# Two heads share one forward substitution in a gated delta rule, and ScalarE takes over sums of squares and copies

## The chip, the core and the metric

The kernel runs on one core of a Trainium2 chip. The core has a matrix engine (TensorE; PE in the profile, with PEld for its weight loads), VectorE (DVE), ScalarE (ACT), GpSimd (POOL), and SyncE (SP), which here only issues DMAs. Each engine executes its own list of instructions in order and waits for semaphores of the others. The metric is the time of one execution on the device, in microseconds (us); lower is better.

## The reference, cut to what matters

A decoder trunk of two layers over 512 positions of width 1024. Layer 0 mixes positions by a gated delta rule with 8 heads of 128, layer 1 by differential attention; each is followed by an MLP of width 4096. The change touches the gated delta rule alone. There, after a projection, a causal convolution and a SiLU, every head has q, k and v of 512 x 128 and two gates per position:

```python
a_mat = jnp.where(strict, jnp.einsum('bhnik,bhnjk->bhnij', kb, kc) * decay, 0.0)
rhs = jnp.concatenate([vc * bc[..., None], kb * jnp.exp(gcum)[..., None]], axis=-1)
sol = lax.linalg.triangular_solve(eye + a_mat, rhs, left_side=True, lower=True, unit_diagonal=True)
...
def step(state, inp):
    qg_i, qk_i, u_i, w_i, kd_i, gl_i = inp
    v_new = u_i - jnp.einsum('bhck,bhkv->bhcv', w_i, state)
    o_i = jnp.einsum('bhck,bhkv->bhcv', qg_i, state) + jnp.einsum('bhij,bhjv->bhiv', qk_i, v_new)
    state = state * gl_i[..., None, None] + jnp.einsum('bhck,bhcv->bhkv', kd_i, v_new)
    return state, o_i
```

A unit lower triangular system is solved for every chunk of positions, and a recurrence runs over the chunks. q and k are divided by their norms, and the output of each head goes through an RMS norm and a gate before the output projection.

## The kernel before, in words

The residual is held transposed, model dimension on partitions. Matrix products with weights are made as three fp32r products (high x high, high x low, low x high; `three`, lines 299 to 302). ACT rounds a weight tile to its high part (`wh`, line 293), and POOL or DVE makes the low part (`wl`, line 284). One modulation weight tile per two weight tiles is also reduced on DVE in this stage (line 193).

The delta rule works on four chunks of 128 positions per head. One head passes through these steps:

- `proj_head` (line 490): three projections into three banks of tag `j`; the causal convolution of q, k and v (ACT line 481, DVE line 483), SiLU (line 485). The results kT, qT and vT take three of the 9 buffers `cv`.
- `gdn` up to its first yield, first the decay matrix `ex` (lines 524 to 535). k is transposed and copied to `kn` (line 539, 3 buffers). Its sum of squares is made by `sumsq`: one square of 128x512 on ACT (line 518), one reduction on DVE (line 520). From it come the factors `rk` (POOL, line 543) and `sj`. The products k k and k q scaled by them are `bq` (line 558, 6 buffers, two per head).
- The unit triangular 128x128 matrices are inverted by blocks. The diagonal 16x16 blocks of the four chunks, 32 blocks, are compacted into `dc` (line 574). They go through DRAM (`d1`, line 576) into `mt` with one block per partition (line 578). There a forward substitution, 15 steps of a multiply and a subtract on DVE (lines 584 and 586), makes the inverses `xv`. They go through DRAM again (`d2`, line 589; `tc`, line 591) and are spread into `t` (line 593).
- Three doubling levels (16 to 32, 32 to 64, 64 to 128; lines 596 to 639) make the inverse of 128 out of those of 16. They use products on PE with tag `i` (two banks), copies `um` (lines 607 and 624, one buffer) and subtractions on DVE (lines 614, 615, 635 and 638). `t` and its transpose `z` are updated.
- v is transposed and scaled (`vn`, line 648), and q's sum of squares gives `rq`.
- From the first yield to the second, the recurrence over the four chunks (lines 667 to 691) in one bank `r`. Per chunk: `r` from the state (line 676), a product with `z`, the copy `y` to SBUF on DVE (line 681), then the products of `y` with `kn` (line 683, first three chunks) and with the attention part of `bq` (line 684), the output part `o` and the state `st`.
- After the second yield, the norm of `o` and its transposition into `oT`.

The program emits the heads one after the other: `proj_head(h)`, the whole of `gdn(h)` up to the second yield, then the rest of head h-1 (lines 729 to 735). The gate's projections follow (lines 737 and 738). This order isn't that of the engines: the tile framework plans the lists from it when the kernel is built. Among the instructions whose operands and buffers it expects to be ready it takes the earliest of the program first, so work of later heads stands between the steps of earlier ones. A buffer is given to the next tile of its tag when the last reader of the old one is done. All weight and block transfers are issued by SP in one order.

Of the kernel before, what the change touches and what calls it, by code (L numbers as in the profile page):

```python
# [22 lines left out]
H = 8  # L23
# [62 lines left out]
def trunk_kernel(ctx: ExitStack, tc: tile.TileContext, a, outT):  # L86
# [141 lines left out]

    mhalf = cp.tile([P, 8], F32, name="mhalf")
    G.memset(mhalf, -0.5)  # L230
    eye = cp.tile([32, SUB, SUB], F32, name="eye")
    nc.scalar.dma_start(eye, a["eye"])

    FULL, HALVES = slice(0, S), (slice(0, 256), slice(256, 512))
# [271 lines left out]

    m_sub = mask[:, M_L1:M_L1 + P]

    def gdn(h):
        def natural(src, tag="a"):  # L510
            ps = bank(tag)
            for c in range(NT):
# [2 lines left out]

        def sumsq(src, tag):
            sq = big(g_pool, {"sqq": "sqk"}.get(tag, tag), 1)
            A.activation(sq, src, AF.Square)
            ss = col(4, tag)
            V.tensor_reduce(out=ss, in_=v3(sq), axis=AX.X, op=ALU.add)  # L520
            return ss


# [50 lines left out]
        V.tensor_reduce(out=dc, in_=db.rearrange("p (u b c) -> p u c b", u=4, c=SUB), axis=AX.X, op=ALU.add)  # L574
        d1 = dp.tile([4, P, SUB], F32, tag="d1", name=nm("d1"))
        nc.sync.dma_start(d1.rearrange("u p c -> p u c"), dc)
        mt = g_pool.tile([32, SUB, SUB], F32, tag="mt", name=nm("mt"), bufs=2)
        nc.sync.dma_start(mt.rearrange("p r c -> p (r c)"), d1.rearrange("u (b r) c -> (u b) (r c)", r=SUB))
        xv = g_pool.tile([32, SUB, SUB], F32, tag="xv", name=nm("xv"), bufs=2)
        pr = g_pool.tile([32, SUB, SUB], F32, tag="pr", name=nm("pr"), bufs=2)  # L580
        G.tensor_copy(xv, eye)
        for s in range(SUB - 1):
            shp = [32, SUB - 1 - s, s + 1]
            V.tensor_tensor(out=pr[:, s + 1:, :s + 1], in0=mt[:, s, s + 1:].unsqueeze(2).to_broadcast(shp),
                            in1=xv[:, s, :s + 1].unsqueeze(1).to_broadcast(shp), op=ALU.mult)
            V.tensor_tensor(out=xv[:, s + 1:, :s + 1], in0=xv[:, s + 1:, :s + 1], in1=pr[:, s + 1:, :s + 1],
                            op=ALU.subtract)
        d2 = dp.tile([32, SUB * SUB], F32, tag="d2", name=nm("d2"))
        nc.sync.dma_start(d2, xv.rearrange("p r c -> p (r c)"))
        tc_ = g_pool.tile([P, 4, SUB], F32, tag="tc", name=nm("tc"), bufs=2)  # L590
        nc.sync.dma_start(tc_, d2.rearrange("(u b) (r c) -> (b r) u c", u=4, r=SUB))
        t_ = big(g_pool, "t", 2)
# [23 lines left out]
        for b in (32, 64):  # L616
            parts = [(slice(lo, lo + b), slice(lo + b, lo + 2 * b)) for lo in ((0, 64) if b == 32 else (0,))]
            pu = bank("i")
            um = big(g_pool, "um", 1)
            for p0, p1 in parts:  # L620
                for n in range(4):
                    T.matmul(pu[p1, n * b:(n + 1) * b], lhsT=B(n)[p0, p1], rhs=uu(t_, n)[p0, p0], start=True, stop=True)
            for p0, p1 in parts:
                V.tensor_copy(um[p1, 0:4 * b], pu[p1, 0:4 * b])
            pz = bank("i")
            for p0, p1 in parts:
                for n in range(4):
                    T.matmul(pz[p0, n * b:(n + 1) * b], lhsT=um[p1, n * b:(n + 1) * b], rhs=uu(z, n)[p1, p1],
                             start=True, stop=True)
            if b == 32:  # L630
                p0, p1 = parts[0]
                for n in range(4):
                    T.matmul(pz[p1, n * b:(n + 1) * b], lhsT=uu(z, n)[p1, p1], rhs=um[p1, n * b:(n + 1) * b],
                             start=True, stop=True)
                V.tensor_tensor(out=v3(t_)[p1, :, p0], in0=v3(t_)[p1, :, p0],
                                in1=v3(pz[p1, 0:4 * b], b), op=ALU.subtract)
            for p0, p1 in parts:
                V.tensor_tensor(out=v3(z)[p0, :, p1], in0=v3(z)[p0, :, p1], in1=v3(pz[p0, 0:4 * b], b),
                                op=ALU.subtract)
# [27 lines left out]
        for c in range(NT):  # L667
            r = uu(vn, 0)
            if c > 0:
                T.matmul(R(3), lhsT=uu(kT[h], c), rhs=st, start=True, stop=True)  # L670
                if c > 1:
                    out(c - 1)
                else:
                    A.activation(uu(o, 0), R(2), AF.Copy)
                r = g_pool.tile([P, P], F32, tag="r", name=nm("r"), bufs=2)
                V.scalar_tensor_tensor(out=r, in0=R(3), scalar=neg[:, c, h:h + 1], in1=uu(vn, c),
                                       op0=ALU.mult, op1=ALU.add)
                T.matmul(R(1), lhsT=uu(qT[h], c), rhs=st, start=True, stop=True)
            T.matmul(R(2), lhsT=uu(z, c), rhs=r, start=True, stop=True)
            y = g_pool.tile([P, P], F32, tag="y", name=nm("y"), bufs=2)  # L680
            V.tensor_copy(y, R(2))
            if c < NT - 1:
                T.matmul(R(0), lhsT=uu(kn, c), rhs=y, start=True, stop=True)
            T.matmul(R(2), lhsT=ATT(c), rhs=y, start=True, stop=True)
            if c > 0:
                A.activation(uu(o, c), R(1), AF.Copy, scale=eg[:, c, h:h + 1])
            if c == 0:
                V.tensor_copy(st, R(0))
            elif c < NT - 1:
                V.scalar_tensor_tensor(out=st, in0=st, scalar=gl[:, c, h:h + 1], in1=R(0), op0=ALU.mult, op1=ALU.add)  # L690
# [35 lines left out]
        queue[c - 17][1].insert(0, lambda c=c: mod_bias(c - 8, c))  # L726
    rate[0] = 0.5
    heads = []
    for h in range(H):
        proj_head(h)  # L730
        heads.append(gdn(h))
        next(heads[h])
        next(heads[h])
        if h:
            next(heads[h - 1], None)
    rate[0] = 0.5
    for i in range(0, H, 2):
        gate(i, 2)
# [225 lines left out]
def host_inputs(inp):  # L964
    f = {k: np.asarray(v) for k, v in inp.items()}

    def cl(v):
        return v.reshape(-1, P).T

    conv = f["a_conv_w"][0].reshape(4, 24, P).transpose(2, 1, 0).reshape(P, 96)  # L970
    packed = np.concatenate(
        [cl(f["mod_b"]), cl(f["kv_mod_b"]), cl(f["norm_mix_g"]), cl(f["norm_mlp_g"]), cl(f["kv_norm_g"]),
         cl(f["final_g"]), conv, cl(f["a_out_norm_g"]), cl(f["b_subln_g"]), cl(f["b_lambda"])], axis=1)
    assert packed.shape == (P, N_COLS)
    r = {
        "xT": f["x"][0].T,
        "cols": packed,
        "masks": host_masks(),
        "rope": host_rope(),
        "eye": np.tile(np.eye(SUB, dtype=np.float32)[None], (32, 1, 1)),  # L980
        "c": f["c"],
        "a_log": f["a_log"],
        "a_dt_bias": f["a_dt_bias"],
        "mod_wT": f["mod_w"].transpose(0, 2, 1).reshape(12288, D),
        "kv_mod_wT": f["kv_mod_w"].T,
        "a_w_in": f["a_w_in"][0],
        "a_w_out": f["a_w_out"][0],
        "kv_w": f["kv_w"],
        "b_w_q": f["b_w_q"][0],
        "b_w_out": f["b_w_out"][0],  # L990
        "mlp_w1": f["mlp_w1"],
        "mlp_w2": f["mlp_w2"],
    }
    return {k: np.ascontiguousarray(v) for k, v in r.items()}
# [16 lines left out]
```

## Time and profile before

| | |
|---|---|
| median of 3 runs | 1387.76 us (1387.6 to 1387.95) |
| profiled execution, its own time | 1388.69 us |
| its span | 1386.9 us, granted TensorE clock 0.983 |
| PE busy / weight loads | 1314.4 us (95%) / 1112.8 us (80%) |
| DVE, ACT, POOL busy | 851.1, 529.3, 472.0 us |
| stage of the delta-rule heads | from about 70 to 390 us |

A busy PE isn't a PE at its peak: matmuls are pipelined, and the records overlap. A row of a group gives engine, line, operation, tiles and shapes, the count, the busy time in all, the mean of one in ns, and the idle time of the engine before them with what ended it. A row of the timeline begins with start and duration in us. A row of the waits reads: who waited for whom, us in all, times, the longest.

### The profile page before, as it was taken

What the parts mean: (1) busy time and instruction counts of PE and PEld (TensorE: products, weight loads), DVE (VectorE), ACT (ScalarE), POOL (GpSimd) and SP (SyncE); (2) the same over time, 40 slices, a digit from 0 to 9 for tenths busy, and PEclk for the clock granted to TensorE, in tenths of its full rate; (3) what the DMA queues carried; (4) which work ended last, traced back from release to release, by engine and by line L of the source; (5) the groups of instructions that cost most, each with busy time, mean ns of one, the idle gap of its engine ahead of it and who ended that gap; (6) DMA issues with size and microseconds to landing.
All of it is one profiled execution on the core that took longest, in us unless ns stands there. A gap on an engine that the chain in (4) does not pass through costs nothing. (4 is left out here: it accounts for less than half of the span.)

```text
span 1386.9 us, 19590 instructions
## 1 busy us (share of the span) xinstructions
PE 1314.4 (95%) x7432; PEld 1112.8 (80%) x7432; DVE 851.1 (61%) x1688; ACT 529.3 (38%) x951; POOL 472.0 (34%) x281
## 2 busy tenths in 40 slices
PE   4886998999999999999999999999999999999997
PEld 3665887777779888888889988888798888888897
DVE  6989888899856987778861587777552110031113
ACT  3394344443424533225332354444344322143221
POOL 3324132222003544444444112232135444444441
PEclk9997999999999999999999999999999999999998
DMA  9632322224541776766742233211113233232221
GB/s 313 212 88 51 83 77 72 77 73 138 174 165 62 258 242 226 241 233 218 239 169 100 81 99 103 65 65 66 61 62 121 92 97 101 91 105 93 92 76 61
DMA packets 113213, 174.98 MB, mean 126 GB/s; under 512 B 16384, under 2 KB 56992, under 8 KB 113120
## 3 DMA queue, kind: packets, MB, share of 16 engines
q1 hardware_dynamic: 112416, 172.92, 38.7%
q8 instruction: 58, 0.95, 0.3%
q10 hardware_dynamic: 704, 0.83, 0.2%
q14 instruction: 35, 0.29, 0.1%
HBM read 170.04 MB, written 2.62 MB: 124 GB/s over the span
## 5 line engine op out<-in xcount | busy, mean ns | idle before, releaser
L284 POOL TENSOR_TENSOR wl<-raw,wh 128x1024 fp32r<-128x1024 f32 (+1 forms) x137 | 329.6, 2406 | 395.4 <-ACT wh L293 395.4
L293 ACT ACTIVATE wh<-raw 128x1024 fp32r<-128x1024 f32 (+2 forms) x217 | 216.0, 996 | 505.4 <-PE pj L301 253.4
L300 PE MATMUL pj<-h,wh 128*128 128x512 f32 (+1 forms) x816 | 290.7, 360 | 16.4 <-DVE cv L483 7.4
L301 PE MATMUL pj<-h,wh 128*128 128x512 f32 (+1 forms) x816 | 292.0, 358 | 0.0
L302 PE MATMUL pj<-h,wl 128*128 128x512 f32 (+1 forms) x816 | 290.0, 357 | 0.7 <-DVE wl L284 0.7
L193 DVE SCALAR_TENSOR_TENSOR mw<-mw,one,cs 128x1024 f32<-128x1024 f32 x96 | 210.1, 2202 | 47.5 <-ACT one L213 47.2
L300 PEld LDWEIGHTS pj<-h,wh 128*128 128x128 f32 x816 | 155.8, 192 | 37.9 <-ACT h L278 7.9
L302 PE MATMUL pj<-u,wl 128*128 128x512 f32 (+1 forms) x512 | 172.2, 336 | 0.0
L301 PE MATMUL pj<-u,wh 128*128 128x512 f32 (+1 forms) x512 | 172.2, 336 | 0.0
L300 PE MATMUL pj<-u,wh 128*128 128x512 f32 (+1 forms) x512 | 172.1, 336 | 0.0
L302 PEld LDWEIGHTS pj<-h,wl 128*128 128x128 f32 x816 | 156.5, 192 | 19.0 <-DVE wl L284 1.9
L301 PEld LDWEIGHTS pj<-h,wh 128*128 128x128 f32 x816 | 156.8, 192 | 17.9 <-DVE h L279 0.3
L346 DVE SCALAR_TENSOR_TENSOR x<-pj,mod,x 128x256 f32<-128x256 f32 (+1 forms) x53 | 30.3, 585 | 156.0 <-PE pj L302 156.0
L300 PEld LDWEIGHTS pj<-u,wh 128*128 128x128 f32 x512 | 97.2, 190 | 10.3 <-issue 0.2
L301 PEld LDWEIGHTS pj<-u,wh 128*128 128x128 f32 x512 | 97.2, 190 | 10.1
L302 PEld LDWEIGHTS pj<-u,wl 128*128 128x128 f32 x512 | 97.2, 190 | 9.9
L284 DVE TENSOR_TENSOR wl<-raw,wh 128x1024 fp32r<-128x1024 f32 (+2 forms) x80 | 83.7, 1047 | 18.0 <-ACT wh L293 17.9
L767 DVE SCALAR_TENSOR_TENSOR pj<-pj,r 128x512 f32<-128x512 f32 x32 | 21.6, 690 | 52.2 <-ACT r L766 52.0
L300 PE MATMUL pn<-h,wh 128*128 128x512 f32 x128 | 49.8, 389 | 0.0
L301 PE MATMUL pn<-h,wh 128*128 128x512 f32 x128 | 49.8, 389 | 0.0
L302 PE MATMUL pn<-h,wl 128*128 128x512 f32 x128 | 49.8, 389 | 0.0
L300 PE MATMUL pm<-h,wh 128*128 128x512 f32 x128 | 49.8, 389 | 0.0
(298 smaller groups left out, 2377.1 us busy)
## 6 DMA issues: line engine op xcount, KB each, us to landing
raw<-in_mlp_w_dram SPq DMA_DIRECT2D x128, 512.0 KB, 3.6
mw<-in_mod_wT_dram SPq DMA_DIRECT2D x96, 512.0 KB, 4.7
raw<-in_a_w_in_dram SPq DMA_DIRECT2D x96, 128.0 KB, 2.6
mw<-in_kv_mod_wT_dram SPq DMA_DIRECT2D x16, 512.0 KB, 5.1
raw<-in_kv_w_dram SPq DMA_DIRECT2D x16, 512.0 KB, 3.3
x<-in_xT_dram SPq DMA_DIRECT2D x16, 256.0 KB, 5.7
raw<-in_a_w_in_dram SPq DMA_DIRECT2D x16, 256.0 KB, 2.9
raw<-in_a_w_out_dram SPq DMA_DIRECT2D x8, 512.0 KB, 4.3
```

The costliest lines, as they stand in the source:

```text
L193: V.scalar_tensor_tensor(out=w, in0=w, scalar=one, in1=cs, op0=ALU.mult, op1=ALU.mult, accum_out=raw_mod[:, c:c + 1])
L284: (V if n else G).tensor_tensor(out=out, in0=x, in1=hi.bitcast(F32), op=ALU.subtract)
L293: A.activation(wh, raw, AF.Copy)
L300: T.matmul(ps, lhsT=wh, rhs=xh, start=first, stop=False, skip_group_check=skip)
L301: T.matmul(ps, lhsT=wh, rhs=xl, start=False, stop=False, skip_group_check=skip)
L302: T.matmul(ps, lhsT=wl, rhs=xh, start=False, stop=last, skip_group_check=skip)
L346: V.scalar_tensor_tensor(out=x[d][:, sl], in0=ps[j][:, sl], scalar=mod[:, gt + d:gt + d + 1], in1=x[d][:, sl], op0=ALU.mult, op1=ALU.add)
L767: V.scalar_tensor_tensor(out=ps[j], in0=ps[j], scalar=0.0, in1=r, op0=ALU.max, op1=ALU.mult)
```

## The change

Three things change.

The forward substitution leaves `gdn` and becomes `blocks_inv`, once for two heads, on 64 partitions: head h0 writes its blocks to the lower 32 partitions of a common `mt`, head h0+1 to the upper 32. A new first yield stands behind the DMA that fills `mt`. The program's order is now, per pair: projection and first part of the one head, the same of the other, the common substitution, then rest of the first part and recurrence of the one, closing part of the head before it, and the same for the other. Numbers of buffers other than that of `pr` (2 to 1) stay; `eye` has 64 partitions.

`sumsq` makes four squares of 128x128 on ACT, each with an accumulated sum, in place of one square of 128x512 and a reduction on DVE.

The copies `um` of the second and third doubling levels and `y` of the recurrence go from DVE to ACT.

```diff
-    eye = cp.tile([32, SUB, SUB], F32, name="eye")
+    eye = cp.tile([64, SUB, SUB], F32, name="eye")
...
-    def gdn(h):
+    def blocks_inv(inv):
+
+        mt = inv["mt"]
+        xv = inv["xv"] = g_pool.tile([64, SUB, SUB], F32, tag="xv", name=nm("xv"), bufs=2)
+        pr = g_pool.tile([64, SUB, SUB], F32, tag="pr", name=nm("pr"), bufs=1)
+        G.tensor_copy(xv, eye)
+        for s in range(SUB - 1):
+            shp = [64, SUB - 1 - s, s + 1]
+            V.tensor_tensor(out=pr[:, s + 1:, :s + 1], in0=mt[:, s, s + 1:].unsqueeze(2).to_broadcast(shp),
+                            in1=xv[:, s, :s + 1].unsqueeze(1).to_broadcast(shp), op=ALU.mult)
+            V.tensor_tensor(out=xv[:, s + 1:, :s + 1], in0=xv[:, s + 1:, :s + 1], in1=pr[:, s + 1:, :s + 1],
+                            op=ALU.subtract)
+
+    def gdn(h, inv, part):
...
-            A.activation(sq, src, AF.Square)
             ss = col(4, tag)
-            V.tensor_reduce(out=ss, in_=v3(sq), axis=AX.X, op=ALU.add)
+            for c in range(NT):
+                A.activation(uu(sq, c), uu(src, c), AF.Square, accum_out=ss[:, c:c + 1])
...
-        mt = g_pool.tile([32, SUB, SUB], F32, tag="mt", name=nm("mt"), bufs=2)
-        nc.sync.dma_start(mt.rearrange("p r c -> p (r c)"), d1.rearrange("u (b r) c -> (u b) (r c)", r=SUB))
-        xv = g_pool.tile([32, SUB, SUB], F32, tag="xv", name=nm("xv"), bufs=2)
-        pr = g_pool.tile([32, SUB, SUB], F32, tag="pr", name=nm("pr"), bufs=2)
...
+        nc.sync.dma_start(inv["mt"][part].rearrange("p r c -> p (r c)"), d1.rearrange("u (b r) c -> (u b) (r c)", r=SUB))
+        yield
         d2 = dp.tile([32, SUB * SUB], F32, tag="d2", name=nm("d2"))
-        nc.sync.dma_start(d2, xv.rearrange("p r c -> p (r c)"))
+        nc.sync.dma_start(d2, inv["xv"][part].rearrange("p r c -> p (r c)"))
...
-                V.tensor_copy(um[p1, 0:4 * b], pu[p1, 0:4 * b])
+                A.activation(um[p1, 0:4 * b], pu[p1, 0:4 * b], AF.Copy)
...
-            V.tensor_copy(y, R(2))
+            A.activation(y, R(2), AF.Copy)
...
-    for h in range(H):
-        proj_head(h)
-        heads.append(gdn(h))
-        next(heads[h])
-        next(heads[h])
-        if h:
-            next(heads[h - 1], None)
+    for h0 in range(0, H, 2):
+        inv = {"mt": g_pool.tile([64, SUB, SUB], F32, tag="mt", name=nm("mt"), bufs=2)}
+        for h in (h0, h0 + 1):
+            proj_head(h)
+            heads.append(gdn(h, inv, slice(32 * (h - h0), 32 * (h - h0) + 32)))
+            next(heads[h])
+        blocks_inv(inv)
+        for h in (h0, h0 + 1):
+            next(heads[h])
+            next(heads[h])
+            if h:
+                next(heads[h - 1], None)
```

More of the change, by code (lines that the diff above doesn't have):

```diff
@@ L576, in gdn @@
         nc.sync.dma_start(d1.rearrange("u p c -> p u c"), dc)
-        mt = g_pool.tile([32, SUB, SUB], F32, tag="mt", name=nm("mt"), bufs=2)
-        nc.sync.dma_start(mt.rearrange("p r c -> p (r c)"), d1.rearrange("u (b r) c -> (u b) (r c)", r=SUB))
-        xv = g_pool.tile([32, SUB, SUB], F32, tag="xv", name=nm("xv"), bufs=2)
-        pr = g_pool.tile([32, SUB, SUB], F32, tag="pr", name=nm("pr"), bufs=2)
[L581 to L587, printed above, removed]
+        nc.sync.dma_start(inv["mt"][part].rearrange("p r c -> p (r c)"), d1.rearrange("u (b r) c -> (u b) (r c)", r=SUB))
+        yield
         d2 = dp.tile([32, SUB * SUB], F32, tag="d2", name=nm("d2"))
-        nc.sync.dma_start(d2, xv.rearrange("p r c -> p (r c)"))
+        nc.sync.dma_start(d2, inv["xv"][part].rearrange("p r c -> p (r c)"))
         tc_ = g_pool.tile([P, 4, SUB], F32, tag="tc", name=nm("tc"), bufs=2)
@@ L979, in host_inputs @@
         "rope": host_rope(),
-        "eye": np.tile(np.eye(SUB, dtype=np.float32)[None], (32, 1, 1)),
+        "eye": np.tile(np.eye(SUB, dtype=np.float32)[None], (64, 1, 1)),
         "c": f["c"],
```

## The prediction

> **What bounds the kernel now.** I read the totals first, then the sums over stretches.
>
> ```profile
> span 1386.9 us, 19590 instructions
> PE 1314.4 (95%) x7432; PEld 1112.8 (80%) x7432; DVE 851.1 (61%) x1688; ACT 529.3 (38%) x951; POOL 472.0 (34%) x281
> ...
> 70.00:150.00 80.00, 63.42 (x337) 49.25 (x336) 68.66 (x187) 47.75 (x82) 24.17 (x20) 0.87 0.29 79
> 150.00:390.00 240.00, 227.35 (x1559) 184.49 (x1558) 209.29 (x601) 102.78 (x190) 52.03 (x40) 0.99 0.35 102
> 400.00:420.00 20.00, 20.00 (x140) 18.76 (x139) 10.07 (x17) 5.98 (x10) 0.00 (x0) 1.00 0.34 122
> ```
>
> The columns behind each length are PE, PEld, DVE, ACT, POOL, then the granted clock. From 400 us on PE is the bound (20.00 of 20 us in the last row), and the change touches little of what follows. The delta-rule heads run from 70 to about 390 us. There DVE is busy 278 of 320 us (87%), ACT only 151. Time gained or lost is decided in this stage, and it reaches the end in full, since PE has a full queue of work behind it.
>
> PE's 95% from 150 to 390 looks as if 12.7 us were all there is to win. PEld is busy 77% there and 94% from 400 to 420, where PE never waits, so up to 18% of the stage is slack. (The Trainium skill, "Trainium Kernel Development and Optimization", Performance Expectations, says so in general: matmul busy time is a bad measure of the distance to the roofline, since matmuls overlap, and weight-load time a good one. The two rows above agree; by PE's row alone a gain over 12.7 us after 150 us would be impossible.)
>
> What PE waits for there:
>
> ```profile
> PE pj L300 <- DVE cv L483: 4.0, 3, 2.0
> PE pi L598 <- DVE t L593: 3.0, 4, 1.9
> ```
>
> Both are DVE's: the convolutions that free the projection's banks, and `t`, which follows the substitution.
>
> The pace of the heads is seen best in one row per head, the first `y` copy of its recurrence (heads 0, 1, 4, 5, 6, 7 here), with the steps of heads 5 to 7 between:
>
> ```profile
> 147.74 0.28 DVE L681 COPY y<-pr 128x128 f32<-128x128 f32 x1
> ...
> 167.94 0.27 DVE L681 COPY y<-pr 128x128 f32<-128x128 f32 x1
> ...
> 267.76 0.60 ACT L539 ACTIVATE kn<-pa 128x512 f32<-128x512 f32 x1 [0.28 <-PE pa L513]
> ...
> 273.64 0.27 DVE L681 COPY y<-pr 128x128 f32<-128x128 f32 x1
> ...
> 282.84 0.38 PE L683 MATMUL pr<-y,kn 128*128 128x128 f32 x2
> 283.14 1.05 DVE L574 TENSOR_REDUCE dc<-db 128x64 f32<-128x512 f32 x1
> 284.22 0.37 SPq L576 DMA_DIRECT2D d<-dc  x1
> 285.99 0.33 SPq L578 DMA_DIRECT2D mt<-d  x1
> 288.61 0.15 DVE L586 TENSOR_TENSOR xv<-xv,pr 32x15 f32<-32x15 f32 x1
> 289.58 0.17 DVE L586 TENSOR_TENSOR xv<-xv,pr 32x15 f32<-32x15 f32 x1
> 296.72 0.67 DVE L593 TENSOR_TENSOR t<-tc,mask 128x512 f32<-128x512 f32 x1
> 310.75 0.27 DVE L681 COPY y<-pr 128x128 f32<-128x128 f32 x1
> 320.75 0.15 DVE L586 TENSOR_TENSOR xv<-xv,pr 32x15 f32<-32x15 f32 x1
> 326.59 0.67 DVE L593 TENSOR_TENSOR t<-tc,mask 128x512 f32<-128x512 f32 x1
> 340.58 0.29 DVE L681 COPY y<-pr 128x128 f32<-128x128 f32 x1
> ...
> 373.71 0.28 DVE L681 COPY y<-pr 128x128 f32<-128x128 f32 x1
> ```
>
> From head 1 to head 7 the step is (373.71 - 167.94) / 6 = 34.3 us, **68.6 us for two heads**. Head 6's substitution runs from 289.58 to 320.90, 31.3 us: other DVE work stands between its operations.
>
> **The change part by part: DVE and ACT.**
>
> ```profile
> L584 DVE TENSOR_TENSOR pr<-mt,xv 32x15 f32<-32x15 f32 (+7 forms) x120 | 27.1, 233 | 0.3
> L586 DVE TENSOR_TENSOR xv<-xv,pr 32x15 f32<-32x15 f32 (+7 forms) x120 | 23.3, 201 | 0.3
> L681 DVE COPY y<-pr 128x128 f32<-128x128 f32 x32 | 9.1, 283 | 2.8 <-PE pr L679 2.5
> L624 DVE COPY um<-pi 32x128 f32<-32x128 f32 (+1 forms) x24 | 8.1, 336 | 10.0 <-PE pi L622 9.5
> L520 DVE TENSOR_REDUCE sqk<-sqk 128x4 f32<-128x512 f32 x8 | 5.4, 670 | 4.9 <-ACT sqk L518 4.9
> ...
> L914 ACT ACTIVATE on<-po 128x256 f32<-128x256 f32 x16 | 6.1, 380 | 4.7 <-PE po L302 4.6
> L518 ACT ACTIVATE sqk<-kn 128x512 f32<-128x512 f32 x8 | 5.0, 626 | 0.1
> L914 ACT ACTIVATION_READ_ACCUMULATOR on<-po 128x1 f32 x16 | 3.2, 198 | 0.0
> L674 ACT ACTIVATE o<-pr 128x128 f32<-128x128 f32 x8 | 2.2, 276 | 15.1 <-PE pr L670 15.1
> ```
>
> A copy takes as long on 32 partitions (the L624 group) as on 128 (L681), by its elements, so I cost a substitution operation on 64 partitions like one on 32. Half of the 240 go: (27.1 + 23.3) / 2 = 25.2 us. The 24 reductions of L520 (8 are in the row) save 3 x 5.4 = 16.2, the `y` copies 9.1, the `um` copies 8.1. Together 58.6 us of DVE's 278. Were the stage as long as now, DVE would fall from 87% to (278 - 58.6) / 320 = 69% busy.
>
> ACT gains 24 x (4 squares of 128 and 4 reads of the accumulator, less one square of 512). A 128-square is not in the trace: between 0.276 (a 128 copy) and 0.380 (a 256-square); I take 0.28, and 24 x (4 x 0.28 + 4 x 0.198 - 0.626) = 31 us; at 0.38 it is 40. The copies add 32 x 0.276 = 9 and about 7 for `um`. ACT goes from 151 to some 198 us of 320: room, and the work lies beside PE's. Were there none, each sum's 1.3 to 1.7 us, less the 0.67 of the reduction, would lengthen a head's step. A `y` copy costs the path nothing by its length (0.276 for 0.283) but now queues in ACT's order behind weight roundings and table loads; behind it wait both products that read `y`, and through them the state. I take 0.
>
> A rule speaks against this part: the Trainium skill, "ScalarE: Activation LUTs", Rules for kernel authors, puts simple arithmetic on VectorE, and its section on table loads gives 186 ns plus 0.833 ns per element, some 293 ns for 128 elements, an estimate from that page. The trace agrees within 0.02 us at 128 and at 512. By the page's figure the term would be 32 for 31, so the sum stays.
>
> **The ring that the pairing makes.** `kn` has 3 buffers and `bq` those of 3 heads. Heads 0 and 1 hold two each until their recurrences; head 2 takes the third. Head 3's `kn` therefore waits for the third state product of head 0's recurrence, and the common substitution of 2 and 3 waits for head 3. Today only the head itself waits like that, and in the rows it doesn't: head 7's `kn` comes 17.5 us after head 4 let go (300.71, quoted below, less 283.22). In the pair the steps stand in a ring, one turn for two heads:
>
> 1. First `y` of the pair to that product: 273.64 to 282.84 + 0.38, **9.6**.
> 2. `kn` to `mt` landed, with these rows:
>
> ```profile
> 300.71 0.59 ACT L539 ACTIVATE kn<-pa 128x512 f32<-128x512 f32 x1
> ...
> 317.97 0.33 SPq L578 DMA_DIRECT2D mt<-d  x1
> ...
> DMA to landing us min/median/max: 1.6/1.6/2.3
> ```
>
> Head 6: 267.76 to 285.99 + 1.6, 19.8; head 7: 18.9. Of this the two copies through DRAM are 284.22 to 287.59, 3.4, and `dc` 1.05; the rest is mostly queueing. I take **17**: the sum of squares itself is 4 x 0.48 instead of 0.63 + 0.67, 0.6 longer, but DVE's queue is shorter by the reductions, and no other head's substitution stands in between.
> 3. The substitution, 30 dependent operations.
>
> ```profile
> 106.77 0.16 DVE L584 TENSOR_TENSOR pr<-mt,xv 32x15 f32<-32x15 f32 x1
> ...
> 124.42 0.28 DVE L586 TENSOR_TENSOR xv<-xv,pr 32x15 f32<-32x15 f32 x2
> ...
> 347.97 0.18 DVE L584 TENSOR_TENSOR pr<-mt,xv 32x39 f32<-32x39 f32 x1
> 348.18 0.19 DVE L586 TENSOR_TENSOR xv<-xv,pr 32x39 f32<-32x39 f32 x1
> ```
>
> Alone, one follows another at 0.21, so 30 take 6.3; head 6 took 31.3; head 0, which goes ahead of all others' work as the pair's now will, 17.9. I take **15**, nearest to head 0 and a little under, with DVE less full.
> 4. Last operation to `t`: 288.76 to 296.72 is 8.0, 320.90 to 326.59 is 5.7: 6.8, and one more DMA issue of 0.3 ahead of it: **7.1**.
> 5. `t` through the three doubling levels to the next first `y`: 296.72 to 310.75 and 326.59 to 340.58: **14.0**.
>
> Sum 62.7 against 68.6. Three such turns lie between head 1 and head 7: 3 x (62.7 - 68.6) = **-17.7 us**. At the start the pair waits for head 1's data:
>
> ```profile
> 113.37 0.32 SPq L578 DMA_DIRECT2D mt<-d  x1
> ```
>
> 113.37 + 1.6 + 15 + 7.1 + 14 = 151.1 for head 0's first `y`, 3.4 later than 147.74; but head 1, ready beside it, need not stay 20.2 us behind, so head 1 stands where it stood: 0. The larger `eye` is loaded before the stage; the halved `xv` copies are POOL's, which has room: 0.
>
> The profiled execution took 1388.69 us, 1.8 round its span: 1388.69 - 17.7 = 1371.0. It lies 0.9 over the median of the runs, 1387.76, so I forecast **1370 us**. With substitutions of 11 to 20 us the case reaches from 1357 to 1384.
>
> **The rivals.**
>
> *The ring turns slower than today.* One common chain must be fed by the later head, where today two heads' chains overlap. If step 3 stays as stretched as for head 6 (27 of its 31.3) and step 2 stays at 19, a turn is 9.6 + 19 + 27 + 7.1 + 14 = 76.7: 3 x 8.1 = +24, **1412 us**. It decides once steps 2 and 3 together pass 37.9. For it: head 6's own two steps are 19.8 + 31.3 = 51. Against it: those ran on a DVE at 87%, and behind other heads' work.
>
> *PE becomes the bound.* If DVE's release shortens the steps further, a turn ends at what PE needs: 184.49 / 240 against 18.76 / 20 is 82% of 68.6, 56 us, so -37 and **1350 us**. For it: PE's longest waits name DVE; with the lone chain of 6.3 the ring would turn in 54. Against it: PE's order is fixed ahead, and steps 4 and 5 don't shrink.
>
> *Nothing is seen.* The ring turns in about 68 us: what DVE gives up ACT takes, in whose order the sums, `y` and `um` now wait. **1387 us**. For it: steps that depend on each other, not busy engines, would then set the pace; against it: ACT stays under two thirds.
>
> **How the numbers follow.** The forecast gets 0.43, PE as the bound 0.13, nothing 0.10, the slower ring 0.34. Under 0.2%, 2.8 us, a difference couldn't be told from none. Faster 0.56, same 0.10, slower 0.34. The range runs from 1345, a little under PE's bound, to 1416, where the slower half of the ring's case is left out.
>
> **What would show it.** Right: first `y` rows that come in twos about 15 us apart, and two twos some 63 us apart; a first operation of each common chain within 30 us of the `y` of the pair before; chains of 11 to 20 us; DVE near 75% from 150 us on. Wrong: pairs 69 us or more apart, with chains over 21 us or a `kn` that isn't waiting for the recurrence; long idle times of DVE ended by ACT's `y`, `um` or squares; or PE without slack between two pairs.

## The result, and the profile after

The changed kernel takes **1400.49 us** (median of 4 runs, 1398.57 to 1402.57), the kernel before 1387.86 us in the same comparison (4 runs, 1387.6 to 1389.03). The ratio is 1.0098 (95% interval 1.0079 to 1.0117): 1% slower. The forecast was 1370 us, so its sign is wrong. The time lies in the range that was given, between the rivals "nothing is seen" (1387 us) and the slower ring (1412 us).

The totals and the sums over stretches of the changed kernel, with the same columns as before (length, PE, PEld, DVE, ACT, POOL, granted clock):

```profile
span 1398.3 us, 19652 instructions
PE 1317.5 (94%) x7432; PEld 1114.8 (80%) x7432; DVE 815.0 (58%) x1488; ACT 559.3 (40%) x1175; POOL 472.8 (34%) x277
...
70.00:150.00 80.00, 66.83 (x309) 53.43 (x308) 64.16 (x141) 54.14 (x122) 27.19 (x18) 0.87 0.39 105
150.00:390.00 240.00, 219.43 (x1523) 177.99 (x1522) 172.79 (x430) 119.97 (x351) 46.75 (x36) 0.96 0.32 90
400.00:420.00 20.00, 16.36 (x80) 12.29 (x80) 9.47 (x21) 7.67 (x17) 2.36 (x2) 1.00 0.46 155
```

The work moved as planned, though less of it vanished than was reckoned: DVE is busy for 815.0 us in all, 36.1 less than before and not 58.6. DVE has 64.16 + 172.79 = 237 us of work from 70 to 390 us instead of 278, and ACT 174 instead of 151. PE gets less done in the stage than before (219.43 for 227.35 from 150 to 390), and from 400 to 420 it isn't full yet (16.36 for 20.00): the heads haven't ended there.

The places where one pair hands over to the next, rows picked from the timelines of the changed kernel's engines (start, duration, engine and line). The first `y` copies are those of heads 0, 1, 2, 4, 6 and 7; the rows between them follow heads 2 and 3, 4 and 5, 6 and 7 through the ring:

```profile
115.22 0.17 DVE L517 TENSOR_TENSOR pr<-mt,xv 64x15 f32<-64x15 f32 x1
139.69 0.15 DVE L519 TENSOR_TENSOR xv<-xv,pr 64x15 f32<-64x15 f32 x1
158.12 0.27 ACT L685 ACTIVATE y<-pr 128x128 f32<-128x128 f32 x1
166.95 0.49 PE L687 MATMUL pr<-y,kn 128*128 128x128 f32 x2
167.53 0.60 ACT L552 ACTIVATE kn<-pa 128x512 f32<-128x512 f32 x1
174.07 0.28 ACT L685 ACTIVATE y<-pr 128x128 f32<-128x128 f32 x1 [0.45 <-PE pr L683]
185.81 0.17 DVE L517 TENSOR_TENSOR pr<-mt,xv 64x15 f32<-64x15 f32 x1
213.61 0.15 DVE L519 TENSOR_TENSOR xv<-xv,pr 64x15 f32<-64x15 f32 x1
233.63 0.27 ACT L685 ACTIVATE y<-pr 128x128 f32<-128x128 f32 x1
242.87 0.38 PE L687 MATMUL pr<-y,kn 128*128 128x128 f32 x2
243.29 0.60 ACT L552 ACTIVATE kn<-pa 128x512 f32<-128x512 f32 x1 [0.85 <-PE pr L687]
261.04 0.17 DVE L517 TENSOR_TENSOR pr<-mt,xv 64x15 f32<-64x15 f32 x1
290.35 0.15 DVE L519 TENSOR_TENSOR xv<-xv,pr 64x15 f32<-64x15 f32 x1
310.36 0.27 ACT L685 ACTIVATE y<-pr 128x128 f32<-128x128 f32 x1
319.37 0.38 PE L687 MATMUL pr<-y,kn 128*128 128x128 f32 x2
319.79 0.60 ACT L552 ACTIVATE kn<-pa 128x512 f32<-128x512 f32 x1 [0.53 <-PE pr L687]
336.41 0.17 DVE L517 TENSOR_TENSOR pr<-mt,xv 64x15 f32<-64x15 f32 x1
351.62 0.17 DVE L519 TENSOR_TENSOR xv<-xv,pr 64x15 f32<-64x15 f32 x1
372.88 0.28 ACT L685 ACTIVATE y<-pr 128x128 f32<-128x128 f32 x1
393.45 0.26 ACT L685 ACTIVATE y<-pr 128x128 f32<-128x128 f32 x1
```

The pairs turn in 233.63 - 158.12 = 75.5, then 76.7, then 62.5 us; two heads took 68.6 before. The last head's first `y` comes at 393.45 instead of 373.71, 19.7 us later. The `kn` of heads 3, 5 and 7 starts 0.04 to 0.09 us after the end of the third state product of heads 0, 2 and 4 (166.95 + 0.49 = 167.44, then 167.53): the ring that the prediction described is there. The common substitutions run for 24.6, 28.0, 29.5 and 15.4 us.

What stands between the operations of one of these chains, the third, on the timelines of DVE and POOL (a part, with other work's rows kept):

```profile
261.98 1.05 POOL L541 TENSOR_TENSOR gm<-mask,g_hi 128x512 fp32r<-128x512 f32 x1 [1.53 <-PE pa L545]
261.99 1.07 DVE L519 TENSOR_TENSOR xv<-xv,pr 64x15 f32<-64x15 f32 x1
...
268.56 0.20 DVE L517 TENSOR_TENSOR pr<-mt,xv 64x48 f32<-64x48 f32 x1
268.68 1.27 DVE L193 SCALAR_TENSOR_TENSOR mw<-mw,one,cs 128x1024 f32<-128x1024 f32 x1
...
270.08 0.19 DVE L519 TENSOR_TENSOR xv<-xv,pr 64x48 f32<-64x48 f32 x1
270.20 0.94 DVE L284 TENSOR_TENSOR wl<-raw,wh 128x768 fp32r<-128x768 f32 x1
271.07 0.20 DVE L517 TENSOR_TENSOR pr<-mt,xv 64x55 f32<-64x55 f32 x1
```

An operation of 0.2 us is followed by one on a weight tile, of 0.94 or 1.27 us, and only then by the next of the chain. Thirty operations that would need 6 us alone so need nearly 30. In the 29.5 us of this chain DVE also does eleven operations on weight tiles (10.3 us) and ten of the convolutions of later heads (7.4 us); in the 15.4 us of the last chain, behind which no head is left, seven on weight tiles (5.9 us) and no convolution. DVE isn't evenly filled: the sums over equal stretches of the changed kernel show that it is half empty while the pair waits for its later head and full while the chain runs (third figure behind the length).

```profile
140.00:180.00 40.00, 36.65 (x290) 30.55 (x288) 20.23 (x51) 13.86 (x46) 3.67 (x4) 0.90 0.14 37
180.00:220.00 40.00, 33.54 (x162) 27.16 (x161) 36.33 (x90) 26.35 (x72) 13.88 (x12) 0.92 0.47 123
220.00:260.00 40.00, 38.83 (x318) 31.54 (x317) 21.59 (x56) 17.89 (x65) 5.63 (x6) 1.00 0.07 18
260.00:300.00 40.00, 34.05 (x168) 27.69 (x167) 33.22 (x83) 21.57 (x48) 12.38 (x8) 0.91 0.42 115
```

DVE works 20.23, 36.33, 21.59 and 33.22 of 40 us, the DMA share and its GB/s (last two columns) go up and down with it, and PE goes the other way (36.65, 33.54, 38.83, 34.05). The second and third chain begin at 185.81 and 261.04; SP issues no transfer at all from 145.8 to 180.7 and from 220.1 to 257.0 us, so the weight tiles' work comes with the chain. Where the 19.7 us end is seen at the first activation of the MLP, in the group of each kernel (the kernel before first):

```profile
L766 ACT ACTIVATE r<-pj x32: 580/596/604, 454.0 to 1286.9; 128x512 f32<-128x512 f32 x32
```

```profile
L775 ACT ACTIVATE r<-pj x32: 580/596/604, 467.2 to 1298.4; 128x512 f32<-128x512 f32 x32
```

It starts 13.2 us later (467.2 - 454.0), about the 12.6 us by which the time grew. So 19.7 of delay at the last head became 13.2 at the MLP. PE had worked ahead while it waited: up to head 7's first `y` it has done 2025 of the 2515 matmuls that precede the MLP's first activation, in the kernel before 1988 of them, so 490 are left instead of 527.

### The profile page after: what moved, and what is told of

Read it like the earlier page. It is cut to its first block, busy times and chain, and to the rows that moved or that the text cites. A ratio compares the mean times of both kernels' runs of the same rounds, so it can differ in the third digit from the quotient of the medians.

```text
span 1398.3 us, 19652 instructions
## 1 busy us (share of the span) xinstructions
PE 1317.5 (94%) x7432; PEld 1114.8 (80%) x7432; DVE 815.0 (58%) x1488; ACT 559.3 (40%) x1175; POOL 472.8 (34%) x277
## 5 line engine op out<-in xcount | busy, mean ns | idle before, releaser
L300 PEld LDWEIGHTS pj<-h,wh 128*128 128x128 f32 x816 | 157.1, 193 | 50.1 <-issue 10.3
L300 PEld LDWEIGHTS pj<-u,wh 128*128 128x128 f32 x512 | 97.2, 190 | 10.3 <-issue 0.2
L301 PEld LDWEIGHTS pj<-u,wh 128*128 128x128 f32 x512 | 97.2, 190 | 10.1
```

The lines of the kernel that those rows point to most:

```text
L300: T.matmul(ps, lhsT=wh, rhs=xh, start=first, stop=False, skip_group_check=skip)
L301: T.matmul(ps, lhsT=wh, rhs=xl, start=False, stop=False, skip_group_check=skip)
```

## The experiments

In the first eight the question is which part of the change costs the time, and by what. Theory: the ring of the pair, with its buffers, its common chain and the later head. Rivals: ScalarE's new work; the order on SP, which issues the block transfers among the weight loads. In the others the buffers and ScalarE's parts are taken one by one. Each edit makes the planner write a new order for the engines, so a kernel differs from its neighbour by more than the lines shown. The kernel before ran along with each group of experiments; its medians lie between 1386.61 and 1387.86 us, so times of different groups compare to about 1 us.

**1. The pairs alone.** The ScalarE part is undone in the changed kernel:

```diff
+            A.activation(sq, src, AF.Square)
-            for c in range(NT):
-                A.activation(uu(sq, c), uu(src, c), AF.Square, accum_out=ss[:, c:c + 1])
+            V.tensor_reduce(out=ss, in_=v3(sq), axis=AX.X, op=ALU.add)
...
-                A.activation(um[p1, 0:4 * b], pu[p1, 0:4 * b], AF.Copy)
+                V.tensor_copy(um[p1, 0:4 * b], pu[p1, 0:4 * b])
...
-            A.activation(y, R(2), AF.Copy)
+            V.tensor_copy(y, R(2))
```

> Pairs with one substitution, but sums of squares, um and y stay on VectorE. Theory (the ring of the pairing costs the time: kn of a pair's second head waits for the recurrence of the pair before, then the stretched common substitution follows): still slower than before, 1398 to 1425 us, first y copies of the pairs 74 us or more apart, common substitutions of 24 to 35 us, since VectorE has more other work to put between their operations. Rival (ScalarE's new work in the steps costs the time): the time falls back to 1388 us or under, pairs 69 us or less apart.

Measured: 1424.28 us (1416.82 to 1425.94), ratio to the kernel before 1.0258 (1.0229 to 1.0286). The pairing by itself costs about 37 us, and ScalarE's part takes back 24 of them. The common chains last 26.0, 26.7, 27.4 and 21.9 us, the turns 78.7, 76.6 and 72.5, so the last of each is a little under what was expected. Head 1 to head 7 need (408.8 - 180.0) / 6 = 38.1 us each.

**2. ScalarE's part alone.** In the kernel before, with heads one by one, sums, `um` and `y` go to ScalarE (the lines of experiment 1 the other way round).

> Single heads as before, with sums of squares, um and y on ScalarE. Theory of the ring: no ring, VectorE has some 33 us less to do in a stage where it is 87% busy, so faster, 1365 to 1384 us, heads 31 to 34 us apart. Rival (ScalarE's new work costs the time): slower, 1395 to 1405 us, heads 35.5 us or more apart.

Measured: 1372.69 us, ratio 0.9896 (0.9881 to 0.9911), faster than both kernels; the heads come 30.9 us apart. With experiment 1 this settles the sign: ScalarE's work isn't the cost, the pairing is. On top of ScalarE's part the pairing costs 1400.49 - 1372.69 = 27.8 us.

**3. Both rings opened.** The changed kernel with a fourth `kn` and `bq` for four heads. The room comes from one buffer less for the modulation weights and one `xv` instead of two.

```diff
-MWB = 4
+MWB = 3
...
-        xv = inv["xv"] = g_pool.tile([64, SUB, SUB], F32, tag="xv", name=nm("xv"), bufs=2)
+        xv = inv["xv"] = g_pool.tile([64, SUB, SUB], F32, tag="xv", name=nm("xv"), bufs=1)
...
-        kn = big(g_pool, "kn", 3)
+        kn = big(g_pool, "kn", 4)
...
-        bq = [big(g_pool, "bq", 6) for _ in range(2)]
+        bq = [big(g_pool, "bq", 8) for _ in range(2)]
```

> The changed kernel with kn in 4 and bq in 8 buffers, so that the second head of a pair needs no buffer of the pair before (space made by 3 instead of 4 buffers of modulation weights and 1 instead of 2 of xv). Theory of the ring: the first part of the second head no longer waits for a recurrence, kn of heads 3, 5 and 7 come well before the third state product of heads 0, 2 and 4, pairs come less than 70 us apart and the time falls to 1360 to 1388 us. Rival (ScalarE's work, or something in the pair's own chain): the time stays at 1395 to 1405 us.

Measured: 1375.43 us, ratio 0.9915 (0.9900 to 0.9930). The `kn` copies of heads 3, 5 and 7 on this kernel's timeline, with head 0's third state product behind the first:

```profile
143.47 0.60 ACT L552 ACTIVATE kn<-pa 128x512 f32<-128x512 f32 x1 [1.68 <-PE pa L526]
169.07 0.38 PE L687 MATMUL pr<-y,kn 128*128 128x128 f32 x2
...
219.69 0.60 ACT L552 ACTIVATE kn<-pa 128x512 f32<-128x512 f32 x1
...
290.87 0.60 ACT L552 ACTIVATE kn<-pa 128x512 f32<-128x512 f32 x1
```

Head 3's copy now starts 26 us before the end of that product instead of 0.09 us behind it; head 5's and head 7's come 4.4 and 0.7 us before the products that held them. Of the pairing's 27.8 us, 25.1 are gone, so the lock between a pair's later head and the recurrence of the pair before is what the time went into. The turns show two ways in which it did. In the first the chain takes 30.2 us, longer than the 28.0 of the changed kernel, and still the turn falls from 75.5 to 51.5 us: there a long chain costs little, since the next pair's first half doesn't wait for the recurrence. The second turn falls from 76.7 to 66.7, by as much as its chain gets shorter (19.3 us for 29.5). The third is longer than before, 66.0 for 62.5, with a chain of 15.7. DVE's work is spread more evenly with the rings open, 29.0, 32.6, 31.5 and 25.4 of 40 us in the stretches from 140 to 300. Even so the paired kernel gains nothing over the single heads of experiment 2.

(The Trainium skill, "Perfetto Trace Analysis", Optimization Strategy, says that the same gap repeating on the engine that should be saturated can mean too little space for the next tile. This case agrees: PE was busy only 33.54 and 34.05 of 40 us in the stretches after the first two locks, the next tile's write sat 0.09 us behind the old one's last reader, and one more `kn` and two more `bq` took 25 us out.)

**4. A short chain.** The changed kernel makes 5 of the 15 steps of the substitution; the other ten are left out, so the inverses are incomplete.

```diff
-        for s in range(SUB - 1):
+        for s in range(5):
```

> The changed kernel with 5 of the 15 steps of the forward substitution; the other 10 are left out. Theory of the ring with the substitution as its stretched step: chains of 6 to 11 us instead of 16 to 30, a turn 13 to 20 us shorter, so some 3 x 13 to 3 x 20 us less: 1345 to 1365 us. Rival (the substitution is not on the path, ScalarE's work is): 20 operations of 0.13 us in each of 4 chains are some 10 us of VectorE's work beside the path, the time falls by 0 to 8 us, 1392 to 1400 us.

Measured: 1378.09 us, ratio 0.9930 (0.9912 to 0.9948), less gain than expected. The chains last 7.2, 2.7, 6.6 and 6.2 us. First `y` of heads 0 and 2, head 2's third product and head 5's `kn` on the timeline:

```profile
141.73 0.27 ACT L685 ACTIVATE y<-pr 128x128 f32<-128x128 f32 x1
...
194.23 0.28 ACT L685 ACTIVATE y<-pr 128x128 f32<-128x128 f32 x1
202.76 0.49 PE L687 MATMUL pr<-y,kn 128*128 128x128 f32 x2
...
224.46 0.60 ACT L552 ACTIVATE kn<-pa 128x512 f32<-128x512 f32 x1
```

The first turn holds the second chain. It falls from 75.5 to 52.5, near the 50.2 of the ring's sum (75.5 less 28.0 - 2.7). The second turn is 75.7, nearly as before, for another reason: `kn` comes 21 us after its buffer is free (224.46 - 203.25), since head 5's projection and convolution end late. The third is 68.6, longer than in the changed kernel, with head 7's `kn` 16 us after its buffer is free. What made the projections late, the run doesn't tell; SP's long waits before block transfers (21.2 us up to 166.6, 16.9 us up to 235.5) end well before head 5's copy, or after it. So the ring sets the pace only as long as the next head's projection is ready when the ring lets go. DVE also has 80 operations less to do here; that the gain comes from the shorter chain rests on the first turn, not on the time.

**5. Block transfers away from SP.** In the changed kernel GpSimd issues the transfers into and out of `d1`, so that no weight load stands behind a wait for a pair's blocks.

```diff
-        nc.sync.dma_start(d1.rearrange("u p c -> p u c"), dc)
-        nc.sync.dma_start(inv["mt"][part].rearrange("p r c -> p (r c)"), d1.rearrange("u (b r) c -> (u b) (r c)", r=SUB))
+        nc.gpsimd.dma_start(d1.rearrange("u p c -> p u c"), dc)
+        nc.gpsimd.dma_start(inv["mt"][part].rearrange("p r c -> p (r c)"), d1.rearrange("u (b r) c -> (u b) (r c)", r=SUB))
```

> The changed kernel with the two transfers that bring the diagonal blocks to mt (d1 and mt) issued by GpSimd instead of SP; buffers as changed. In the changed kernel SP stood 88 us before d1 while weight loads queued behind it. Theory A (the late blocks cost the time because SP's order holds back the weights behind them): weights come on time, the time falls by most of the 28 us between the pairs and single heads, to 1372 to 1388 us, with the same three kn buffers. Theory B (the ring over kn and the substitution costs it by itself): heads 3, 5 and 7 still get kn with the third state product of heads 0, 2 and 4, pairs still 70 us or more apart, 1393 to 1402 us.

Measured: 1404.38 us, ratio 1.0138 (1.0123 to 1.0153), 2.4 us over theory B's range. The wait of SP's queue that goes away is this one of the changed kernel, before the transfer into `d1` on line 589 (us in all, times, longest):

```profile
SPq L589 <- DVE kd L648: 88.3, 5, 37.0
```

With it gone, the `kn` of heads 3, 5 and 7 still start within 0.1 us of the end of the product that held them, head 3's here:

```profile
169.57 0.60 ACT L552 ACTIVATE kn<-pa 128x512 f32<-128x512 f32 x1 [0.91 <-PE pr L687]
```

The loads now wait in that queue for free weight tiles (163.8 us, 42.1 in one piece before the third chain) instead, and still come with the chains, which last 23.7, 28.6, 28.1 and 15.2 us. The pace of the heads is that of the changed kernel, 36.7 us each for 36.6, so the theory of SP's order falls here. One reservation: issuing from GpSimd may have a cost of its own (experiment 7) that hides a small gain.

**6. The common chain on GpSimd.** The 30 operations leave DVE, where other work stands between them.

```diff
-            V.tensor_tensor(out=pr[:, s + 1:, :s + 1], ...
+            G.tensor_tensor(out=pr[:, s + 1:, :s + 1], ...
...
-            V.tensor_tensor(out=xv[:, s + 1:, :s + 1], ...
+            G.tensor_tensor(out=xv[:, s + 1:, :s + 1], ...
```

> The changed kernel with the 30 operations of the common substitution on GpSimd instead of VectorE, where nothing of VectorE's stands between them. Theory B (the ring, with the substitution stretched on VectorE): if GpSimd's chains take 10 to 18 us instead of 24 to 29, turns get 8 to 15 us shorter, 1365 to 1385 us. Theory A (SP's order holds the weights back): SP's wait before d1 stays near 88 us and the time moves little, 1392 to 1402 us.

Measured: 1413.84 us, ratio 1.0199 (1.0183 to 1.0214): a miss, and slower than the changed kernel. The chains did shorten, to 16, 12, 12 and 15 us, but the turns are 63.3, 81.0 and 78.9. Its waits name a new one, PE before the transposition of `t`:

```profile
PE pi L602 <- DVE t L597: 35.5, 4, 12.8
```

PE stands 35.5 us in four pieces for a `t` that comes later than its place in PE's list, and the projection of the next head stands in that list behind it. That the planner had reckoned with a faster chain would explain it; this was only argued.

**7. Block transfers away from SP, single heads.** Experiment 2's kernel with the issues of experiment 5, to see how large SP's part is where there is no pair.

> Single heads with sums of squares, um and y on ScalarE (1372.7 us in its run), d1 and mt issued by GpSimd. There SP waited 46 us before d1 in all, at most 9.9 us at once. Theory A: weights come earlier, a gain of 2 to 8 us, 1364 to 1371 us. Theory B: SP's wait lies off the path, 1370 to 1375 us.

Measured: 1389.48 us (8 runs, 1381.83 to 1398.2), ratio 1.0032 (1.0013 to 1.0050), 17 us more than experiment 2: a miss by both theories. With the issue on GpSimd the kernel is slower and its time scatters, by what isn't shown, so the run says nothing on SP's wait.

**8. Single chains on GpSimd.** Experiment 2's kernel with each head's substitution on GpSimd.

> Single heads with sums of squares, um and y on ScalarE, the substitutions on GpSimd. VectorE loses 240 operations, some 30 us of issue time in the stage. If GpSimd takes under 0.6 us for one and its port costs VectorE little, the heads come closer: 1355 to 1370 us. If GpSimd's operations are slower than 1 us, eight chains of over 30 us set the pace of the heads: 1375 to 1400 us.

Measured: 1420.74 us, ratio 1.0251 (1.0235 to 1.0266): a miss by 50 us. The operation costs what was hoped for. At 306 ns for the multiply and 330 for the subtract a chain takes some 12 us, and yet the heads come 37.5 us apart instead of 30.9. PE's longest waits are before the transposition of `t` again (16.2 us in four pieces from 150 to 390 us, 3.1 in experiment 2). What makes `t` late stays open.

**9 and 10. Each ring by itself.** The changed kernel with the fourth `kn` alone (and one `xv`), and with the eight `bq` alone (with one `xv` and three modulation buffers, which also shows what these two cost).

```diff
-        xv = inv["xv"] = g_pool.tile([64, SUB, SUB], F32, tag="xv", name=nm("xv"), bufs=2)
+        xv = inv["xv"] = g_pool.tile([64, SUB, SUB], F32, tag="xv", name=nm("xv"), bufs=1)
...
-        kn = big(g_pool, "kn", 3)
+        kn = big(g_pool, "kn", 4)
```

> The changed kernel with kn in 4 buffers, bq still in 6 (space from 1 instead of 2 buffers of xv). Theory: two locks hold the second head of a pair, kn (given back with the third state product, 9.5 us after the first y) and bq (its last buffer given back at the end of the recurrence, about 15 us after the first y). With kn open alone, kn of heads 3, 5 and 7 comes early but bq's second half still waits for the end of the recurrence of the pair before; a turn gets 3 to 7 us shorter, 1380 to 1393 us. Rival (kn alone is the lock): as with both opened, 1372 to 1378 us.

```diff
-MWB = 4
+MWB = 3
...
-        xv = inv["xv"] = g_pool.tile([64, SUB, SUB], F32, tag="xv", name=nm("xv"), bufs=2)
+        xv = inv["xv"] = g_pool.tile([64, SUB, SUB], F32, tag="xv", name=nm("xv"), bufs=1)
...
-        bq = [big(g_pool, "bq", 6) for _ in range(2)]
+        bq = [big(g_pool, "bq", 8) for _ in range(2)]
```

> The changed kernel with bq in 8 buffers, kn still in 3 (space as in the run with both: 3 buffers of modulation weights, 1 of xv). Theory: kn stays the lock, kn of heads 3, 5 and 7 still comes with the third state product, 1395 to 1405 us. Rival (bq, or the two changes that make the space, brought the 25 us): 1372 to 1385 us.

Measured: 1390.39 us with `kn` (9 runs; ratio 1.0031, 1.0020 to 1.0041) and 1401.45 us with `bq` (1.0103, 1.0087 to 1.0119). The timeline of experiment 9, head 3's `kn` and its four `bq` writes (the last row holds two), with head 0's last product of the attention part:

```profile
142.21 0.60 ACT L552 ACTIVATE kn<-pa 128x512 f32<-128x512 f32 x1 [1.51 <-PE pa L526]
...
162.31 0.48 DVE L571 SCALAR_TENSOR_TENSOR bq<-pa,sj,ex 128x256 f32<-128x256 f32 x1
164.84 0.48 DVE L571 SCALAR_TENSOR_TENSOR bq<-pa,sj,ex 128x256 f32<-128x256 f32 x1
171.60 0.49 PE L688 MATMUL pr<-y,bq 128*128 128x128 f32 x2 [0.61 <-ACT y L685]
172.88 0.87 DVE L571 SCALAR_TENSOR_TENSOR bq<-pa,sj,ex 128x256 f32<-128x256 f32 x2
```

and that of experiment 10, head 3's `kn`:

```profile
166.91 0.60 ACT L552 ACTIVATE kn<-pa 128x512 f32<-128x512 f32 x1 [0.34 <-PE pr L687]
```

The two locks stand in a row. With `kn` free, `bq` holds head 3: its first write, at 162.31, follows the end of head 0's second attention product (162.28), and its last two wait until head 0's recurrence is over (171.60 + 0.49). With `bq` free, `kn` holds head 3 as before. Freeing `kn` gives 10.1 us, freeing `bq` behind it another 15.0, freeing `bq` alone nothing (+1.0, between overlapping runs). The two smaller buffer numbers, which experiment 10 has too, cost no more than that, so experiment 3's gain belongs to the rings.

**11 and 12. ScalarE's parts, single heads.** The kernel before with only `um` and `y` on ScalarE, and with only the sums there.

```diff
-                V.tensor_copy(um[p1, 0:4 * b], pu[p1, 0:4 * b])
+                A.activation(um[p1, 0:4 * b], pu[p1, 0:4 * b], AF.Copy)
...
-            V.tensor_copy(y, R(2))
+            A.activation(y, R(2), AF.Copy)
```

> Single heads with only um and y on ScalarE. Theory (VectorE's load sets the pace of single heads): some 13 us of VectorE's issue time less, a gain of 4 to 10 us on the kernel before, 1377 to 1383 us. Rival (the copies in ScalarE's order lengthen the recurrence): 1387 to 1395 us.

```diff
-            A.activation(sq, src, AF.Square)
+            for c in range(NT):
+                A.activation(uu(sq, c), uu(src, c), AF.Square, accum_out=ss[:, c:c + 1])
-            V.tensor_reduce(out=ss, in_=v3(sq), axis=AX.X, op=ALU.add)
```

> Single heads with only the sums of squares on ScalarE. Theory (VectorE's load sets the pace): some 14 us of VectorE's issue time less, a gain of 4 to 10 us, 1377 to 1383 us. Rival (four squares and four reads in place of one square hold ScalarE's order): 1387 to 1395 us.

Measured: 1381.88 us (ratio 0.9961, 0.9946 to 0.9976) with the copies, and **1369.47 us** (0.9873, 0.9858 to 0.9887) with the sums, the lowest median of all (its interval overlaps that of experiment 2) and a larger gain than expected. Its heads come 31.4 us apart from head 1 to head 7, instead of 34.3. (The Trainium skill, "Perfetto Trace Analysis", Optimizing Scalar/DVE Operations, says that moving some work to ScalarE may make sense where VectorE is saturated. With DVE at 87% this held, 1.3%.) The copies gain 5.3 us alone (1381.88 against 1387.13 for the kernel before in the same comparison); on top of the sums (experiment 2) no gain of theirs is shown. The sums gain 17.7 us, more than the 16.2 of DVE's rows that they take away; why is open, and a new order of the engines is as good a candidate as a shorter path.

## Why the prediction was wrong, step by step

**What bounds.** That the stage from 70 to 390 us decides, and that what it loses reaches the end, held: 13.2 us at the MLP, 12.6 in the time. "In full" held from the MLP on, not from the last head (19.7).

**The prices of the operations.** Most held. An operation of 15 elements takes 0.15 to 0.17 us on 64 partitions as on 32 where nothing holds it, `y` 0.26 to 0.28 us on ACT. But half of the substitution's operations did not save half of its time, as two groups of the changed kernel show:

```profile
L519 DVE TENSOR_TENSOR xv<-xv,pr 64x15 f32<-64x15 f32 (+7 forms) x60 | 17.0, 284 | 0.3
L517 DVE TENSOR_TENSOR pr<-mt,xv 64x15 f32<-64x15 f32 (+7 forms) x60 | 16.4, 274 | 0.4
```

The means rose from 201 and 233 ns to 284 and 274, so 17.0 us went (50.4 - 33.4) instead of 25.2. Not the partitions did that, as the single rows show, but, as I read it, the company they keep (see the last section). Most of the rest of the gap between 58.6 and 36.1 us lies in the sum of rows: rows overlap (above, the one at 268.68 starts before the one at 268.56 has ended), so a group's sum is more than the busy time it adds. In experiment 2 rows of 33.4 us left DVE, and its busy time fell by 21.6 (851.1 - 829.5). The sum of squares was priced too high: 4 x 0.48. The timeline of the changed kernel shows two squares of one sum, the read of the accumulator between them, 0.31 us apart:

```profile
244.58 0.31 ACT L533 ACTIVATE sqk<-kn 128x128 f32<-128x128 f32 x1
...
244.89 0.29 ACT L533 ACTIVATE sqk<-kn 128x128 f32<-128x128 f32 x1
```

Four take about 1.2 us, less than the 1.30 of the square and the reduction before, and ACT's busy time in the stage rose by 24 us, not 47.

Two slips of the working move nothing. Head 6's substitution begins with a multiply at 288.70, so it took 32.2 us, not 31.3. And 1370 us with substitutions 4 us shorter or 5 longer in three turns gives 1358 and 1385, not 1357 and 1384.

**The ring.** It was described rightly: its lock at `kn` stands in the timeline, and so do its steps. The second lock, at `bq`, whose buffers the prediction counts without putting them into the ring, shows only when `kn` is free (experiment 9). The times of the steps, from the rows quoted above:

| step | forecast | turn 1 | turn 2 | turn 3 |
|---|---|---|---|---|
| 1, first `y` to third product | 9.6 | 9.3 | 9.6 | 9.4 |
| 2, to the substitution | 17 | 18.4 | 17.8 | 16.7 |
| 3, substitution | 15 | 28.0 | 29.5 | 15.4 |
| 4 and 5, to the next `y` | 21.1 | 19.9 | 19.9 | 21.1 |
| turn | 62.7 | 75.5 | 76.7 | 62.5 |

Each step is counted here from the end of the one before, step 2 up to the first operation of the chain. **Step 3 failed**: "I take 15, nearest to head 0 and a little under, with DVE less full." The third turn, with no later pair's work to stand in between, is the forecast to 0.2 us; the first two are the rival's 76.7, within 1.2. At head 7's first `y` the forecast and the measurement lie 17.7 + 19.7 = 37.4 us apart: 26.7 of it in the turns, where step 3 alone is 27.8 over its 3 x 15, and the rest at the start (6.1) and at the last head (4.6). The mean over the stage hid it. DVE's 237 of 320 us are 20 of 40 while the pair waits for its later head and 33 to 36 of 40 while the chain runs, which I read so: one event, the end of the recurrence's hold on the buffers, lets go of the chain and of the other work that had queued up. Within the second and third chain DVE is busy 92% and 94% of the time, in the stretches from the chain before to them 56% and 59%. The even spread of experiment 3, where the hold is gone, fits this reading, and experiment 5 speaks against SP's order as its cause; no run changed DVE's other work alone. The rival's condition, steps 2 and 3 together over 37.9, was met with 46.3 and 47.3. The chain counts in full only because it stands inside the lock: with more buffers (experiment 3) a chain of 30.2 us left a turn of 51.5, and with a chain of 2.7 us (experiment 4) the locked turn fell to 52.5.

**The start.** The first common chain took 24.6 us instead of 15, so head 0's first `y` came at 158.12 instead of 151.1. Head 1's came at 174.07, 6.1 us later than before, where the forecast had 0: head 1 did come closer to head 0 (16.0 us behind instead of 20.2), but less than head 0 was late.

**The sum.** 6.1 at the start and three turns of 372.88 - 158.12 = 214.8 in place of 3 x 68.6 = 205.8 make 15.1; the last head follows its pair's first by 20.6, and not by the 16.0 of head 1, 4.6 more. Together 19.7, as the timeline has it at head 7.

**The rivals.** PE as the bound and "nothing is seen" fell with the turns. The slower ring came true at two turns of three, which is why 1412 was too much. The forecast took the gain to come through the pairing; the pairing loses 28 to 37 us, and ScalarE's part alone gains 14.5.

## What to carry to other kernels

Where two units of work are joined at a common step, count the buffers each of them holds until its release: with three buffers for pairs of two, the later half of a pair waits for the recurrence of the pair before, and a chain that two heads used to overlap then stands in the open. Price such a chain by the other work that its engine gets while it runs, not by the mean of the stage, and take the parts of a change one by one before joining them: here one line of the three (the sums on ScalarE) gained 1.3%, and the pairing lost more than that.

## What the runs showed of the hardware

Small DVE operations and GpSimd's hold each other up. In the third chain's rows above the subtract over 15 elements, 0.15 to 0.20 us at its other seven places in this kernel, took 1.07 us beside a POOL multiply of 1.05 us that had started 0.01 us before it. Over the stage the substitution's operations grew from 201 and 233 ns to 284 and 274, and POOL's multiply of `kn` by `kd`, which falls into the full stretches now, from 1042 to 2022 ns. (The Trainium skill, "SBUF — State Buffer", Who interferes with whom, says that a DVE instruction with two SBUF inputs contends with a GpSimd instruction that reads SBUF, and calls the port pair that they share an exclusive lock. The two rows agree; that all of the growth is this wasn't tested.)

A wait in a DMA queue isn't a cost by its length: SP's 37.0 us before a pair's blocks could be taken away without a change in the heads' pace. And issuing the same small transfers from GpSimd instead of SP made the kernel with single heads 17 us slower, with runs from 1381.83 to 1398.2 us. In the profile, taken in the fastest of these runs, the two transfers of a head land 2.2 and 2.9 us after their issue instead of 1.8 and 2.1; what makes up the 17 us, no run showed.
